# Seven block products in place of eight in two gate/up groups of each FFN, with the weight sums split between VectorE and accumulating DMAs

## The chip, the cores and the metric

The kernel runs on one NeuronCore of a Trainium2 chip. The metric is the device time of one execution in microseconds (us); a run's time is the median of its executions. Engines: TensorE (PE; its weight loads are a row of their own, PEld), VectorE (DVE), ScalarE (ACT), GpSimd (POOL) and SyncE (SP), which only issues DMAs here. Each takes its instructions in a fixed order from a queue of its own. PE writes to PSUM; the others work on SBUF, and DVE and ACT read PSUM too.

## The reference

A decoder trunk of two layers on x of 256 tokens x 1024, in float32:

```
f = swiglu(rms_norm(h, g0)); h = h + 0.5 * rms_norm(f, g1)
h = h + rms_norm(mix(rms_norm(h, g2)), g3)      # layer 0: pooling mixer, layer 1: windowed attention
f = swiglu(rms_norm(h, g4)); h = h + 0.5 * rms_norm(f, g5)
swiglu(h) = (silu(h @ w_gate) * (h @ w_up)) @ w_down     # w_gate, w_up: 1024 x 2816, w_down: 2816 x 1024
```

So there are four FFNs, each read once from HBM. K and V for the attention are projected from h after layer 0.

## The kernel before, in words

The 256 tokens are two row blocks i of 128. Activations are held transposed (`aT`: 8 chunks of 128 of the model dimension, 256 tokens). To keep float32 precision in the fast matmul format (fp32r), each operand is split in two halves: hi, the value cast to fp32r, and lo, the rest. Each product of 128x128 with 128x512 is then three matmuls: hi·hi, hi·lo, lo·hi.

**Weights** arrive as a stream of *units* of 128x1024 float32 (512 KB), in the order of use. `load_unit` (L84) issues the DMA on SP into one of four `raw` buffers, ACT casts the unit to hi (L92), and DVE subtracts to get lo (L93), both into one of eight `hl` buffers. A buffer is free for the next unit when the last matmul that reads it has ended. Everything else on ACT and DVE stands in the same queues between these casts.

**An FFN** (`ffn`, L211) has gate and up in five *groups* of 512 columns and a sixth of 256. A plain group takes gate, 4 units, and up, 4 units: per unit and row block 6 matmuls, so 96 in all. Group 0 comes first: in the first FFN unit by unit for both row blocks, in the others (L250) row block 0 with all eight units and then row block 1. For groups 1 to 4, gate goes to the two `gu` banks of PSUM and up to `acc` banks; `gate` (L216) is silu on ACT, `up` (L221) the product with it on DVE, and `turn` (L226) transposes it on PE (four transposes) and splits it into hi and lo for the down projection. The down projection then takes 22 units, 12 matmuls each; the last six (`TAIL`) are done for row block 0 first, so that its norms begin while PE still works on row block 1.

**A boundary** (`Bound`, L302) follows: `post` (L159) scales the sum by its norm and adds it to h, `norm` (L189) makes the next input, and `transposed` (L175) brings it into the next aT by 8 transposes per row block, ACT's cast (L183) and DVE's subtraction (L184). The power for a norm runs on POOL (L156). PE goes on with row block 0's next matmuls while row block 1 is normalised.

The order on each engine is set by a scheduler when the kernel is built, from the code and its dependences, not by the order of the code alone; each engine then keeps to it.

Of the kernel before, what the change touches and what calls it, by code (L numbers as in the profile page):

```python
# [19 lines left out]
P = 128  # L20
# [7 lines left out]
TAIL = 6  # L28
WARM = 64
CAST = 1024  # L30
# [17 lines left out]
def trunk_kernel(ctx: ExitStack, tc: tile.TileContext, x, pos, gains, pscale, ws, wq, invf, amask, pmat, icnt, out):  # L48
# [6 lines left out]
    s8p = ctx.enter_context(tc.tile_pool(name="s8p", bufs=6))  # L55
# [25 lines left out]
    unit_no = [0]  # L81
    last = {}

    def load_unit():  # L84
        u = unit_no[0]
        unit_no[0] += 1
        raw = rawp.tile([P, 1024], F32, tag="raw", name=f"raw{u}")
        last["dma"] = nc.sync.dma_start(raw, ws[u])
        hl = hlp.tile([P, 2, 1024], F32R, tag="hl", name=f"hl{u}")
        for c in range(0, 1024, CAST):  # L90
            w = slice(c, c + CAST)
            nc.scalar.copy(hl[:, 0, w], raw[:, w])  # L92
            last["dve"] = nc.vector.tensor_sub(hl[:, 1, w], raw[:, w], hl[:, 0, w])  # L93
        return hl

    def load_q_unit(u):
        raw = rawp.tile([P, 1024], F32, tag="raw", name=f"rawq{u}")
        nc.sync.dma_start(raw[:, :768], wq[u])
        hl = hlp.tile([P, 2, 1024], F32R, tag="hl", name=f"hlq{u}")
        nc.scalar.copy(hl[:, 0, :768], raw[:, :768])  # L100
        nc.vector.tensor_sub(hl[:, 1, :768], raw[:, :768], hl[:, 0, :768])
        return hl
# [72 lines left out]
    def transposed(i, src, dst, name):  # L175

        for b in range(2):
            tp = tpp.tile([P, 4, P], F32, tag="tp", name=f"tp_{name}{i}{b}")
            for c in range(4):
                k = b * 4 + c  # L180
                nc.tensor.transpose(tp[:, c], src[:, k * P : (k + 1) * P], ident)
            d = dst[:, :, b * 4 : b * 4 + 4, i * P : (i + 1) * P]
            nc.scalar.copy(d[:, 0], tp)  # L183
            nc.vector.tensor_sub(d[:, 1], tp, d[:, 0])  # L184

# [25 lines left out]
    def ffn(n, aT, boundary, middle=None):  # L211

        h2 = [s8p.tile([P, 2, 4, S], F32R, tag="s8", name=f"h2_{n}_{c}") for c in range(NG + 1)]
        act, prod = {}, {}

        def gate(c, i, g):  # L216
            w = g.shape[-1]
            act[c, i] = sc2.tile([P, 512], F32, tag="w2", name=f"s_{n}_{c}{i}")
            nc.scalar.activation(act[c, i][:, :w], g, AF.Silu)

        def up(c, i, u):  # L221
            w = u.shape[-1]
            prod[c, i] = sc2.tile([P, 512], F32, tag="w2", name=f"m_{n}_{c}{i}")
# [11 lines left out]
        def both(ps, units, c=None):  # L235

            for q in range(4):
                for i in range(2):
                    proj_mm(ps[i], aT, i, units, 512, only=q)
                if c is not None and q < 2:  # L240
                    turn(c, q)

        units = [load_unit() for _ in range(8 - len(first_units))]
        units, first_units[:] = first_units + units, []
# [11 lines left out]
        for c in range(1, NG):  # L256
            units = [load_unit() for _ in range(4)]
            ps = [gup.tile([P, 512], F32, tag="gu", name=f"g_{n}_{c}{i}") for i in range(2)]
            both(ps, units, c - 1)
            for i in range(2):  # L260
                gate(c, i, ps[i])
            units = [load_unit() for _ in range(4)]
            ps = acc_pair(f"u{n}{c}")
            both(ps, units)
            for i in range(2):
                up(c, i, ps[i])
            if c == 2 and middle is not None:
                middle()
        units = [load_unit() for _ in range(4)]
        ps = [gup.tile([P, 512], F32, tag="gu", name=f"g_{n}_{NG}{i}") for i in range(2)]  # L270
        both(ps, units, NG - 1)
        for i in range(2):
            gate(NG, i, ps[i][:, 0:256])
            up(NG, i, ps[i][:, 256:512])

# [7 lines left out]
        for c in range(NF - TAIL):  # L283
            u = load_unit()
            down(c, 0, u)
            down(c, 1, u)
            if c < 2:
                turn(NG, c, 2)
        tail = [load_unit() for _ in range(TAIL)]
# [12 lines left out]
    class Bound:  # L302


        def __init__(self, n, post_idx, half, pre_idx):
            self.n, self.half, self.idx = n, half, (post_idx, pre_idx)

        def prepare(self):
            self.gpost = load_gain(self.idx[0], "post")
            self.gpre = load_gain(self.idx[1], "pre")  # L310
            self.aT = new_aT(self.n)

# [6 lines left out]
        def third(self, i):  # L319
            transposed(i, self.y, self.aT, self.n)  # L320
# [7 lines left out]
    aT = new_aT("x")  # L328
    with tc.manual_schedule(engines={mybir.EngineType.DVE, mybir.EngineType.Activation}):
        y = norm(0, gpre, "x")  # L330
        first_units += [load_unit()]
        nc.sync.dma_start(h[1], x[P:, :])
        transposed(0, y, aT, "x")
        rs = row_rstd(1, "x")
        first_units += [load_unit()]
        y = norm(1, gpre, "x", rs, False)
        first_units += [load_unit()]
        transposed(1, y, aT, "x")
        first_units += [load_unit()]
# [33 lines left out]
    ffn(0, aT, go, rope_tables)  # L373
# [3 lines left out]
    go = Bound("m0", 3, False, 4)  # L377
# [4 lines left out]
    ic = s8p.tile([P, 4, S], F32, tag="s8", name="ic")  # L382
    with in_turn("dma"):
        nc.sync.dma_start(ic, icnt.to_broadcast([P, 4, S]))
    pm = s8p.tile([P, 2, 4, S], F32R, tag="s8", name="pm")
    for si in range(2):
        raw = rawp.tile([P, 1024], F32, tag="raw", name=f"rawpm{si}")
        nc.sync.dma_start(raw, pmat[si])
        nc.vector.tensor_copy(pm[:, si], raw.rearrange("p (g t) -> p g t", g=4))
    u_hl = [s8p.tile([P, 2, D], F32R, tag="s8", name=f"u{i}") for i in range(2)]  # L390
    units = [load_unit() for _ in range(8)]
# [47 lines left out]
    wg += [load_unit() for _ in range(2)]  # L439
# [324 lines left out]
```

## Time and profile before

| | |
|---|---|
| median of 3 timed runs | 992.54 us (991.7 to 993.55) |
| the profiled execution | 995.63 us |
| its span, first to last instruction | 993.7 us |
| busy: PE, DVE, ACT, POOL | 975.3, 575.0, 484.4, 23.2 us |
| moved by DMA | 180.38 MB |

The profile is one execution. "Busy" counts time in instructions; a row of a group gives line, engine, operation, written tile<-read tiles, shape, count, then busy us, mean ns of one, and the idle time of the engine just before them with what ended it. A chain or a timeline gives start and length in us.

### The profile page before, as it was taken

The page shows a single profiled execution, that of the slowest core. Times are in us where ns is not written, and L with a number is a line of the kernel's source. Part 1 is how long each engine was busy: PE and PEld are TensorE (multiplying, and loading weights), DVE is VectorE, ACT ScalarE, POOL GpSimd, SP SyncE. Part 2 cuts the span into 40 slices and gives each one's busy share as a digit, 9 for nine tenths or more (in the row PEclk, how much of TensorE's full clock was granted, in tenths as well). Part 3 has the DMA queues.
Part 4 walks back from the last instruction along what each step waited for, and adds up shares of the span by engine and source line. Part 5 has one row for each costly group of instructions (what it writes and reads, how often), then busy time and mean ns, then how long its engine had stood idle before and what let it go on. Part 6 is the DMA issues. An engine that isn't in the chain of part 4 may idle for free.

```text
span 993.7 us, 12240 instructions
## 1 busy us (share of the span) xinstructions
PE 975.3 (98%) x4664; PEld 810.1 (82%) x4664; DVE 575.0 (58%) x725; ACT 484.4 (49%) x660; POOL 23.2 (2%) x34
## 2 busy tenths in 40 slices
PE   7999999999999999999999999999999999999997
PEld 6888888878788888877888888788898888888886
DVE  5665554578765555447665554685556466555542
ACT  5644443365564444346554443554455565444431
POOL 0000000010100000000000000100000000000000
PEclk8999999999999999999999999999999899999999
DMA  6855655666465575535755756474533137556531
GB/s 224 292 185 188 228 186 189 203 193 213 145 218 185 190 233 180 191 127 174 263 188 171 231 179 197 150 244 154 152 124 128 44 100 260 191 181 203 188 127 42
DMA packets 53722, 180.38 MB, mean 182 GB/s; under 512 B 7265, under 2 KB 7265, under 8 KB 53665
## 3 DMA queue, kind: packets, MB, share of 16 engines
q1 hardware_dynamic: 53584, 179.35, 55.4%
q8 instruction: 36, 0.59, 0.2%
q0 software_dynamic: 80, 0.26, 0.1%
q14 instruction: 22, 0.17, 0.1%
HBM read 178.54 MB, written 1.05 MB: 181 GB/s over the span
## 4 chain that ended last, share of the span: by engine, by line
PE 88%; DVE 4%; issue 3%; ACT 2%; POOL 2%; DMA 1%; SPq 0%; POOLq 0%; DVEq 0%; ACTq 0%
PE g L105 22%; PE acc_d L105 21%; PE acc_u L105 19%; PE acc_b L105 7%; PE vp L105 3%; PE qp L105 3%; PE kp L105 3%; PE htp L230 2%; PE ob L105 1%; PE acc_w L105 1%; PE acc_o L105 1%; DVE h L171 1%; DVE hl L93 1%; ACT hl L92 1%; PE sc L105 1%
## 5 line engine op out<-in xcount | busy, mean ns | idle before, releaser
L93 DVE TENSOR_TENSOR hl<-raw,hl 128x1024 fp32r<-128x1024 f32 x310 | 378.5, 1224 | 298.8 <-ACT hl L92 296.7
L92 ACT CAST hl<-raw 128x1024 fp32r<-128x1024 f32 x310 | 325.5, 1051 | 338.5 <-PE acc_d L105 101.1
L105 PE MATMUL acc_d<-hl,h 128*128 128x512 f32 x1056 | 242.9, 390 | 0.0
L105 PEld LDWEIGHTS acc_d<-hl,h 128*128 128x128 f32 x1056 | 197.4, 188 | 40.7
L105 PE MATMUL g<-hl,aT_m 128*128 128x512 f32 x480 | 116.1, 394 | 0.0
L105 PEld LDWEIGHTS g<-hl,aT_m 128*128 128x128 f32 x480 | 88.6, 188 | 17.8
L105 PE MATMUL acc_u<-hl,aT_m 128*128 128x512 f32 x384 | 88.3, 389 | 0.0
L105 PEld LDWEIGHTS acc_u<-hl,aT_m 128*128 128x128 f32 x384 | 72.1, 188 | 15.0
L105 PE MATMUL acc_u<-hl,aT_f 128*128 128x512 f32 x288 | 67.2, 390 | 0.0
L105 PEld LDWEIGHTS acc_u<-hl,aT_f 128*128 128x128 f32 x288 | 53.8, 188 | 11.5 <-DVE aT_f L184 0.5
L105 PE MATMUL g<-hl,aT_f 128*128 128x512 f32 x240 | 58.7, 395 | 0.0
L105 PE MATMUL g<-hl,aT_x 128*128 128x512 f32 x240 | 58.1, 394 | 0.0
L105 PEld LDWEIGHTS g<-hl,aT_x 128*128 128x128 f32 x240 | 44.3, 188 | 8.9
L105 PEld LDWEIGHTS g<-hl,aT_f 128*128 128x128 f32 x240 | 44.2, 188 | 8.7
L105 PE MATMUL acc_b<-hl,aT_m 128*128 128x512 f32 x192 | 45.3, 392 | 0.1
L105 PE MATMUL acc_u<-hl,aT_x 128*128 128x512 f32 x192 | 44.2, 389 | 0.0
L105 PEld LDWEIGHTS acc_u<-hl,aT_x 128*128 128x128 f32 x192 | 36.0, 188 | 7.5
L105 PEld LDWEIGHTS acc_b<-hl,aT_m 128*128 128x128 f32 x192 | 35.7, 188 | 7.8 <-DVE aT_m L184 0.5
L105 PE MATMUL qp<-hlq,aT_f 128*128 128x384 f32 x192 | 39.1, 346 | 0.0
L105 PE MATMUL kp<-hl,aT_hk 128*128 128x512 f32 x144 | 34.5, 394 | 0.0
L105 PEld LDWEIGHTS qp<-hlq,aT_f 128*128 128x128 f32 x192 | 32.7, 188 | 0.4
L105 PE MATMUL vp<-hl,aT_hk 128*128 128x512 f32 x144 | 33.1, 390 | 0.0
(158 smaller groups left out, 831.3 us busy)
## 6 DMA issues: line engine op xcount, KB each, us to landing
raw<-in_ws SPq DMA_DIRECT2D x310, 512.0 KB, 3.5
rawq<-in_wq SPq DMA_DIRECT2D x16, 384.0 KB, 3.6
gain_post<-in_gains SPq DMA_DIRECT2D x14, 256.0 KB, 4.6
gain_pre<-in_gains SPq DMA_DIRECT2D x12, 256.0 KB, 5.6
rawpm<-in_pmat SPq DMA_DIRECT2D x2, 512.0 KB, 4.7
out_dram<-h SPq DMA_DIRECT2D x4, 256.0 KB, 2.1
h<-in_x SPq DMA_DIRECT2D x2, 256.0 KB, 3.0
h<-in_x SPq DMA_DIRECT2D x1, 512.0 KB, 8.5
```

What stands on the lines that cost most here:

```text
L92: nc.scalar.copy(hl[:, 0, w], raw[:, w])
L93: last["dve"] = nc.vector.tensor_sub(hl[:, 1, w], raw[:, w], hl[:, 0, w])
L105: nc.tensor.matmul(o, l, r, start=start, stop=stop)
L171: nc.vector.scalar_tensor_tensor(h[i][:, c], y[:, c], rs, h[i][:, c], op0=ALU.mult, op1=ALU.add)
L230: nc.tensor.transpose(tp[:, k], prod[c, i][:, k * P : (k + 1) * P], ident)
```

## The change

**The products.** For groups 1 and 3, gate and up of 512 columns are seen as a matrix of 2x2 blocks (rows: the two halves of the model dimension; columns: gate and up), and aT as one of 2x2 blocks (the two row blocks, the two halves). The 2x2 product takes 7 block products instead of 8, with sums of weight blocks and of aT blocks as operands. A block product is 12 matmuls of 128x512; a group takes 84 instead of 96. A `pair` is such a group c and the plain group c+1, whose gate and up are done between the products, two blocks of units at a time.

**The weight sums.** The blocks x, y, z, w (128x2048, 1 MB) give x, x+y, x+y+z, z, y+z, w and x+w (signs are in the stored weights and the sums of aT). x stays in its buffer and is added to in place. The first two sums are DVE additions; sums 2 (y += z) and 3 (x += w) are DMAs from SBUF to SBUF on POOL's queue with an add at the destination. Each operand is cast by ACT and DVE like any block. x and y have two buffers of their own (`xyp`).

**The sums of aT** (`Sums`): four sums of 128x512 with hi and lo, made at the boundary from the transposes in PSUM; they take an `aT` buffer.

**Sizes.** Loads, casts and subtractions go by blocks of two units (128x2048, 1 MB): `raw` 3 blocks (4 units before), `hl` 3 blocks (8 units before). The last group's h2 and other tiles move to half-size buffers. The first four units keep parts of 1024. `kv_input` moves from after group 2 to after the last group (`late`). The stored order of the weights follows. The core of the diff:

```diff
-    rawp = ctx.enter_context(tc.tile_pool(name="rawp", bufs=4))
-    hlp = ctx.enter_context(tc.tile_pool(name="hlp", bufs=8))
+    rawp = ctx.enter_context(tc.tile_pool(name="rawp", bufs=3))
+    xyp = ctx.enter_context(tc.tile_pool(name="xyp", bufs=2))
+    hlp = ctx.enter_context(tc.tile_pool(name="hlp", bufs=3))
...
+    def halves(raw, parts=1, n=1024):
+
+        hl = hlp.tile([P, 2, 2, 1024], F32R, tag="hl", name="hl")
+        for k in range(parts):
+            u = slice(k * (2 // parts), (k + 1) * (2 // parts))
+            nc.scalar.copy(hl[:, 0, u, :n], raw[:, u, :n])
+            last["dve"] = nc.vector.tensor_sub(hl[:, 1, u, :n], raw[:, u, :n], hl[:, 0, u, :n])
+        return [hl[:, :, j] for j in range(2)]
...
+        def product(ps, a, units, start):
+
+            for k in range(4):
+                u = units[k // 2][:, :, (k % 2) * 512 : (k % 2) * 512 + 512]
+                for n, (z, v) in enumerate(((0, 0), (0, 1), (1, 0))):
+                    nc.tensor.matmul(
+                        ps,
+                        a(z, k),
+                        u[:, v],
+                        start=start and k == 0 and n == 0,
+                        stop=k == 3 and n == 2,
+                        skip_group_check=not start,
+                    )
...
+        def add(dst, src, k):
+            if k in DMA_SUMS:
+                nc.gpsimd.dma_start(dst, src, accum_op=ALU.add)
+            else:
+                nc.vector.tensor_add(dst, dst, src)
+
+        def pair(c, turns):
+
+            x, y = [load_raw(1, xyp, "xy") for _ in range(2)]
+            z = load_raw()
+            px = bank()
+            product(px, plain(0, 0), halves(x), True)
+            p1 = temp("p1")
+            nc.scalar.copy(p1, px)
+            add(x, y, 0)
+            py = bank()
+            product(py, summed(0), halves(x), True)
+            p5 = temp("p5")
+            nc.scalar.copy(p5, py)
+            turns[0]()
+            g = [gup.tile([P, 512], F32, tag="gu", name=f"g_{n}_{c}{i}") for i in range(2)]
+            us = load_units(2)
+            both(g, us + us, (0, 1))
+            add(x, z, 1)
+            product(px, summed(1), halves(x), False)
+            u1 = temp("u1")
+            nc.scalar.copy(u1, px)
+            turns[1]()
+            us = load_units(2)
+            both(g, us + us, (2, 3))
...
+            product(py, summed(3), halves(z), False)
+            c01 = temp("c01")
+            nc.vector.scalar_tensor_tensor(c01, py, -1.0, u1, op0=ALU.mult, op1=ALU.subtract)
+            add(y, z, 2)
+            product(px, summed(2), halves(y), False)
+            c11 = temp("c11")
+            nc.vector.scalar_tensor_tensor(c11, px, -1.0, p5, op0=ALU.mult, op1=ALU.subtract)
+            w = load_raw()
+            pz = bank()
+            product(pz, plain(0, 1), halves(w), True)
+            nc.vector.tensor_add(p1, pz, p1)
+            gate(c, 0, p1)
+            up(c, 0, c01)
+            add(x, w, 3)
+            product(px, plain(1, 1), halves(x), False)
+            gate(c, 1, px)
+            up(c, 1, c11)
...
+        pair(1, [lambda: turn(0, 0), lambda: turn(0, 1)])
...
+        pair(3, [turns12, lambda: turn(2, 1)])
```

What this does to the order, at three places. First DVE at the boundary from the first FFN to the mixer, row block 0 (y: post-norm, n: pre-norm, ms: the sum for a norm's power, hl<-raw: a weight's lo half, aT: the next input's). Before:

```order
L171 SCALAR_TENSOR_TENSOR h_94<-y_f_1532,rs_pf_1530,h_94 128x512 x2
L194 TENSOR_TENSOR n_f_1546<-h_94,gain_pre_1167 128x512 x2
L93 TENSOR_TENSOR hl_1675<-raw_1673,hl_1675 128x1024
L154 SCALAR_TENSOR_TENSOR ms_qf_1542<-ss_qf_1537 128x1
L93 TENSOR_TENSOR hl_1680<-raw_1678,hl_1680 128x1024
L195 TENSOR_SCALAR n_f_1546<-n_f_1546,rs_qf_1544 128x512
L93 TENSOR_TENSOR hl_1685<-raw_1683,hl_1685 128x1024
L93 TENSOR_TENSOR hl_1690<-raw_1688,hl_1690 128x1024
L184 TENSOR_TENSOR aT_f_1170<-tp_f_1551,aT_f_1170 128x4x128
```

And now:

```order
L184 SCALAR_TENSOR_TENSOR h_100<-y_f_1421,rs_pf_1419,h_100 128x512 x2
L246 TENSOR_TENSOR n_f_1435<-h_100,gain_pre_1111 128x512 x2
L103 TENSOR_TENSOR hl<-raw_1551,hl 128x2048
L167 SCALAR_TENSOR_TENSOR ms_qf_1431<-ss_qf_1426 128x1
L247 TENSOR_SCALAR n_f_1435<-n_f_1435,rs_qf_1433 128x512
L103 TENSOR_TENSOR hl<-raw_1556,hl 128x2048
L197 TENSOR_TENSOR aT_f_1114<-tp_f_1440,aT_f_1114 128x4x128
```

The same steps in the same order; the weight halves between them are two of 2048 columns, where there were four of 1024, one of them whole between the pre-norm and ms.

Second, PE at the same boundary (tp: the transposes, of row block 0 and then 1; acc_u: the mixer's first projection; pp: its pooling). Before:

```order
L105 MATMUL acc_u_1703<-hl_1675,aT_f_1170 128x512 x6
L105 MATMUL acc_u_1703<-hl_1680,aT_f_1170 128x512 x6
L105 MATMUL acc_u_1704<-hl_1685,aT_f_1170 128x512 x5
L105 MATMUL acc_u_1704<-hl_1690,aT_f_1170 128x512 x6
L181 MATMUL tp_f_1629<-ident,n_f_1624 128x128 x4
L181 MATMUL tp_f_1636<-ident,n_f_1624 128x128 x4
```

And now:

```order
L194 MATMUL tp_f_1440<-ident,n_f_1435 128x128 x4
L194 MATMUL tp_f_1447<-ident,n_f_1435 128x128 x4
L118 MATMUL acc_d_1118<-hl,h_0_5_291 128x512
L118 MATMUL acc_u_1571<-hl,aT_f_1114 128x512 x24
L118 MATMUL acc_u_1572<-hl,aT_f_1114 128x512
L118 MATMUL pp_1660<-pm,u_1549 128x256
L118 MATMUL pp_1674<-pm,u_1549 128x256
L118 MATMUL acc_u_1572<-hl,aT_f_1114 128x512 x2
L194 MATMUL tp_f_1518<-ident,n_f_1513 128x128 x4
L194 MATMUL tp_f_1525<-ident,n_f_1513 128x128 x4
```

Row block 1's transposes now stand behind 27 matmuls of row block 0 and two of the pooling; before there were 36 ahead of them.

Third, DVE at the end of the first pair (raw_584: w; xy_410: x+w; raw_629 and raw_665: the plain blocks of up; xy_724: the next pair's x; c, p, m: see the diff, m being the product with silu). This work has no place in the kernel before, where a group's end on DVE was

```order
L93 TENSOR_TENSOR hl_660<-raw_658,hl_660 128x1024
L224 TENSOR_TENSOR m_10_556<-acc_u_506,s_10_482 128x512
L224 TENSOR_TENSOR m_11_558<-acc_u_507,s_11_484 128x512
L93 TENSOR_TENSOR hl_665<-raw_663,hl_665 128x1024
```

and is now

```order
L103 TENSOR_TENSOR hl<-raw_584,hl 128x2048
L354 SCALAR_TENSOR_TENSOR c_0_564<-st_435,u_0_507 128x512
L103 TENSOR_TENSOR hl<-xy_410,hl 128x2048
L358 SCALAR_TENSOR_TENSOR c_0_582<-st_416,p_0_451 128x512
L103 TENSOR_TENSOR hl<-raw_629,hl 128x2048
L362 TENSOR_TENSOR p_0_432<-st_586,p_0_432 128x512
L103 TENSOR_TENSOR hl<-raw_665,hl 128x2048
L499 CAST posf<-pi_278 128x2
L103 TENSOR_TENSOR hl<-xy_724,hl 128x2048
L280 TENSOR_TENSOR m_0_605<-c_0_564,s_0_603 128x512
```

The product m, which PE's next turn transposes, stands behind the half of the next pair's x.

More of the change, by code (lines that the diff above doesn't have):

```diff
@@ L233, in turn, with both, bank @@
             nc.vector.tensor_sub(d[:, 1], tp[:, :nt], d[:, 0])
-        def both(ps, units, c=None):
-            for q in range(4):
+        def both(ps, units, qs=range(4)):
+            for q in qs:
                 for i in range(2):
                     proj_mm(ps[i], aT, i, units, 512, only=q)
[L240 to L244, printed above, removed]
+        def bank():
+            return accp.tile([P, 512], F32, tag="acc", name=f"st{n}")
@@ L511, in trunk_kernel @@
     for g in range(3):
-        units = [load_unit() for _ in range(4)]
+        units = load_units(4)
         for i in range(2):
@@ L521, in trunk_kernel @@
     for g in range(3):
-        units = [load_unit() for _ in range(4)]
+        units = load_units(4)
         for i in range(2):
@@ L622, in trunk_kernel @@
             values(1, 1)
-    units = [load_unit() for _ in range(4)]
+    units = load_units(4)
     scores(1, 2, gup, "gu")
```

243 lines of the change are left out of this document (156 added, 87 removed).

## Prediction

> **What bounds the kernel now.** I read the page first (parts 1, 2, 4 and 5).
>
> ```profile
> span 993.7 us, 12240 instructions
> ...
> PE 975.3 (98%) x4664; PEld 810.1 (82%) x4664; DVE 575.0 (58%) x725; ACT 484.4 (49%) x660; POOL 23.2 (2%) x34
> ...
> PEclk8999999999999999999999999999999899999999
> ...
> PE 88%; DVE 4%; issue 3%; ACT 2%; POOL 2%; DMA 1%; SPq 0%; POOLq 0%; DVEq 0%; ACTq 0%
> ...
> L93 DVE TENSOR_TENSOR hl<-raw,hl 128x1024 fp32r<-128x1024 f32 x310 | 378.5, 1224 | 298.8 <-ACT hl L92 296.7
> L92 ACT CAST hl<-raw 128x1024 fp32r<-128x1024 f32 x310 | 325.5, 1051 | 338.5 <-PE acc_d L105 101.1
> ```
>
> PE is busy for 975.3 of 993.7 us and carries 88% of the chain that ended last. ACT's casts of the weights wait for PE to give a buffer back, and the subtractions on VectorE (DVE) wait for the casts: both run behind PE. So fewer matmuls are worth their full time, as long as the other engines still keep up everywhere. Next, the chain in order of time inside the second FFN, and one stretch of it by engine (busy us and instructions of PE, PEld, DVE, ACT, POOL, then clock, DMA share, GB/s).
>
> ```profile
> 284.72 2.73 PE g L105 x12
> 287.89 2.79 PE g L105 x12
> 291.11 5.46 PE g L105 x24
> 296.57 10.88 PE acc_u L105 x48
> ```
>
> ```profile
> 296.57:342.00 45.43, 45.43 (x209) 37.60 (x209) 24.41 (x24) 20.95 (x24) 0.00 (x0) 1.00 0.56 187
> ```
>
> A 128x512 matmul passes in 5.46/24 = 0.2275 us, twelve in 2.73. Between the first two pieces lie 287.89 - 284.72 - 2.73 = 0.44 us: one turn (four transposes). In these 45.43 us, two groups long, PE never pauses; DVE works 24.41 us and ACT 20.95.
>
> **What is removed.** Each pair takes 7 products of 12 matmuls for the 96 of a plain group: 12 fewer. Two pairs in four FFNs: 96 x 0.2275 = **-21.8 us**, all on the path. Nothing else leaves PE.
>
> **What DVE and ACT get.** I need prices of 128x2048 instructions, which the trace lacks; I extend them from two lengths.
>
> ```profile
> L184 DVE TENSOR_TENSOR aT_f<-tp_f,aT_f 128x512 fp32r<-128x512 f32 x12 | 7.7, 684 | 2.9 <-ACT aT_f L183 2.9
> L183 ACT CAST aT_f<-tp_f 128x512 fp32r<-128x512 f32 x12 | 6.4, 584 | 0.6 <-PE tp_f L181 0.6
> L219 ACT ACTIVATE s<-g 128x512 f32<-128x512 f32 (+1 forms) x40 | 22.2, 555 | 21.9 <-PE g L105 21.8
> ```
>
> DVE: 684 ns for 512 columns and 1224 for 1024, so 540 more per 512 and 2.30 us for 2048. ACT: 584 and 1051, so 1.99 us. A pair casts 7 blocks of products and 4 plain ones: DVE 11 x 2.30 + two sums of 2.30 + seven short operations and some four turns of 0.68 = 37 us, ACT 11 x 1.99 + about 11 short ones of 0.58 = 28 us. PE needs 180 x 0.2275 + 4 x 0.44 = 42.7 us. DVE is then 87% busy: no bound by itself, but three hl buffers (six units, eight before) leave little slack, so I follow the pair step by step.
>
> **Inside a pair** (us from its first product, no stall assumed). PE: x 0 to 2.7, x+y to 5.5, turn, first plain block to 11.4, x+y+z to 14.1, turn, second plain block to 20.0, z to 22.7, y+z to 25.4, w to 28.2, one matmul, x+w, 23 matmuls, turn at 36.4. A cast may start when the product three blocks back has ended. w: cast behind two silu (20.0 + 0.56), to 22.5, DVE to 24.8, wanted at 25.4. Then c01 to 25.5, the half of x+w (cast from 22.7) to 27.8, c11 to 28.5; but x+w writes the bank that c11 reads, and PE is there at 28.4: stall 0.1. Then DVE has one block to 30.8, p1 to 31.5, one block to 33.8, the next x to 36.1, and the product of c01 and silu to 36.8, which the turn wants at 36.4: stall 0.4. Together 0.5 in 8 pairs: **+4 us**, between 0 (the scales are a few per cent off) and +8.
>
> **Entering a pair.** In FFNs two to four the fourth block of group 0 waits for the first one's buffer until row block 1 has used it, so casts bunch when the pair begins: x+y+z and the second plain block follow each other on ACT at 2 x 1.99 us, where PE has one block of 5.46 us less what it is late. I find PE out of work for some 1.3 us: 3 x 1.3 = **+4 us**, between 1 and 6.
>
> **The two sums by DMA.** No row shows an accumulating DMA. The nearest:
>
> ```profile
> raw<-in_ws SPq DMA_DIRECT2D x310, 512.0 KB, 3.5
> qT<-in_amask POOLq DMA_DIRECT2D x1, 256.0 KB, 5.0
> ```
>
> and the stretch of the first 25 us, 40 slices of GB/s:
>
> ```profile
> GB/s 0 0 3 180 344 321 236 144 177 167 243 347 383 403 419 419 419 419 419 406 229 105 170 334 315 66 39 184 269 374 39 0 85 315 354 53 26 26 177 393
> ```
>
> So the engines move at most 419 GB/s, 2.5 us per MB. A 1 MB load lands in 3.5 + 1.25 = 4.75 us. A sum issued from POOL takes, read once, 5.0 + 0.79/0.419 = 6.9 us; read twice, 5.0 - 0.6 + 5.0 = 9.4; with the two loads that are then in flight taking half of the engines, 11.9. By the Trainium skill ("Collectives: The Full Stack", the bandwidth ceiling) an add in a DMA needs two source reads and so halves the rate (1.93 measured there): by that alone a sum would take some 9.2 us, an estimate, as in the middle case; no run here shows it yet.
>
> y+z has time: it starts when x+y is done, before the pair begins, and is wanted at 14.6. x+w is tight: w's load starts when the first plain block's half is done (DVE does x+y and x+y+z around it: 4.3 to 6.6), lands at 9 to 11.4, and the sum must land by 22.7: 11.3 to 13.7 us for 6.9 to 11.9. I take 0.5 us late per pair: **+4 us**, from 0 to +12; worse is a rival.
>
> **Row boundaries.** Here 2048-wide casts stand where 1024-wide ones stood, on the chain post-norm, pre-norm, transposes. Boundary FFN one to mixer, of before, DVE then PE (start, busy, ..., [idle before <-releaser]), with POOL's power:
>
> ```profile
> 198.20 1.22 DVE L93 TENSOR_TENSOR hl<-raw,hl 128x1024 fp32r<-128x1024 f32 x1
> 199.33 0.15 DVE L154 SCALAR_TENSOR_TENSOR ms_qf<-ss_qf 128x1 f32<-128x1 f32 x1
> ...
> 201.07 0.49 DVE L195 TENSOR_SCALAR n_f<-n_f,rs_qf 128x512 f32<-128x512 f32 x1 [0.44 <-POOL rs_qf L156]
> 201.47 2.52 DVE L93 TENSOR_TENSOR hl<-raw,hl 128x1024 fp32r<-128x1024 f32 x2
> 203.90 1.28 DVE L184 TENSOR_TENSOR aT_f<-tp_f,aT_f 128x512 fp32r<-128x512 f32 x2
> ...
> 212.09 0.49 DVE L195 TENSOR_SCALAR n_f<-n_f,rs_qf 128x512 f32<-128x512 f32 x1 [0.44 <-POOL rs_qf L156]
> ```
>
> ```profile
> 197.14 1.04 ACT L92 CAST hl<-raw 128x1024 fp32r<-128x1024 f32 x1
> 198.08 0.62 ACT L152 ACTIVATE jk_qf<-h 128x512 bf16<-128x512 f32 x1
> ```
>
> ```profile
> 201.70 1.06 PE L181 MATMUL tp_f<-ident,n_f 128*128 128x128 f32 x8 [0.65 <-DVE n_f L195]
> 202.52 1.40 PE L105 MATMUL acc_d<-hl,h 128*128 128x512 f32 x5
> 203.76 8.69 PE L105 MATMUL acc_u<-hl,aT_f 128*128 128x512 f32 x36
> 212.72 1.06 PE L181 MATMUL tp_f<-ident,n_f 128*128 128x128 f32 x8 [0.26 <-DVE n_f L195]
> 213.54 8.43 PE L105 MATMUL acc_u<-hl,aT_f 128*128 128x512 f32 x36
> ```
>
> ACT's cast at 197.14 becomes 1.99 long, jk_qf ends at 199.9, the half of that block holds DVE until 201.5, and only then comes ms_qf (199.33 before). POOL and the way to L195 took 201.07 - 199.33 = 1.74; so L195 starts at 203.2, PE transposes from 203.7 to 204.7 (its tail is through at about 202.2), and behind one more 2.30 us half DVE delivers the first aT at 206.4. PE can do two matmuls before that: row block 0 starts 206.4 - 0.5 - 203.76 = 2.2 us late. Row block 1 follows: its L195 at 213.4 for 212.09, behind another block. But PE now has only 25 matmuls ahead of those transposes, to 211.7, then two of the pooling whose input ACT casts after the normalisation (214.0), then the transposes, to 215.9. Before, 36 were done at 213.54; now 27 and 0.4 us of pooling: (215.9 - 213.54) + 9 x 0.2275 - 0.4 = 4.0 us late. Mixer to FFN two and FFN two to three have the same order of casts (24 to 27 matmuls ahead of the second transposes): 3.2 and 3.5 by the same working. Attention to FFN four still has 36 ahead: 1.2. Sum **+12 us**; at least 4 x 1.2 = 5, at most 4 x 4 = 16. FFN three to the K projections needs no aT at once: nothing.
>
> **The rest.** The mixer, K, V and Q held eight units and hold six: I take +2 (0 to +5). At nothing I cost these. The four sums of aT: their first reader comes after group 0's 22 us of PE; uncovered they would cost some 5 us a boundary. The start: same 1024-wide steps. `kv_input`, moved to the head of the down projections: a block of two units there gives DVE 5.46 us of PE time for 2.30 us of work. SP's queue: the next pair's x stands ahead of raw loads, but takes y's buffer, free at 18.9 us of the pair, so nothing behind it is held; if it took x's own (27.8), the turn would wait some 3 us more. POOL's queue: between the sums of a pair stands nothing, and the powers of the norms come long after the last sum.
>
> **Sum.** -21.8 + 4 + 4 + 4 + 12 + 2 = +4.2 us. The profiled execution took 995.63 us (the span of 993.7 and 1.9 around it), the three timed runs have their median at 992.54, 3.1 lower; on that median: 992.5 + 4.2 = **996.7, so 997 us**.
>
> **Rivals.** (1) *Cover holds: faster.* All edges at the low ends: -21.8 + 0 + 1 + 0 + 5 + 0 = -16; with half of the way from there to my values, -6. So 977 to 990, around 983. For it: PE waits only 0.26 and 0.65 us at these very transposes, and DVE's idle 298.8 us is cover that my step by step may have used too sparingly. Against: 24.41 us of DVE work per 45 become 37. It decides at boundaries of 2 us instead of 3 to 4.
> (2) *The accumulating DMA is the bound: slower.* Place: x+w in each pair; from 12 to 13 us per sum PE stands still for every further us, eight times. At 16 us per sum: 8 x 3.5 = 28 us in place of my 4, so 1021. A longer stop costs more than itself, as the start of the span shows (PE; then the stretch by engine, the clock third from the end):
>
> ```profile
> 10.26 1.09 PE L181 MATMUL tp_x<-ident,n_x 128*128 128x128 f32 x8 [3.65 <-DVE n_x L195]
> ```
>
> ```profile
> 12.00:18.00 6.00, 5.73 (x11) 3.57 (x12) 5.23 (x9) 3.76 (x8) 0.55 (x1) 0.50 0.60 204
> ```
>
> After 3.65 us without work PE has a granted clock of 0.50 for these 6 us, which loses 3 us. At 20 us per sum it would be 8 x (7.5 + 3) = 84 us: 1077. The stops that I forecast, 2.3 us at the longest, stay under that length. The Trainium skill ("TensorE: Matmul & The Clock Gate", part 1) puts the limit at an idle window of about 3.4 us, after which the clock is halved until some 3.4 us of steady work: by that, too, my sum pays nothing for the clock, and the trace agrees with 3.65 us. For it: no row gives its price, and 5.0 us for 256 KB from POOL is already slow beside 3.5 for 512 KB from SP. Against: y+z shows a slack of ten us, and the engines move 187 of 419 GB/s here. The Trainium skill ("SBUF — State Buffer", who interferes with whom) says that a VectorE instruction with two SBUF inputs holds up GpSimd instructions that read SBUF, not those that only write it, as writing descriptors does; by that DVE's load alone would not make this rival true. No run shows it yet.
> (3) *Nothing in sum*: edges of 20 to 24 us, 990.6 to 994.5.
>
> **How the numbers follow.** My sum, slower: 0.36, its own range 994.6 to 1006. Rival 1: 0.39. Rival 2: 0.14. Rival 3: 0.11. A measurement of this kernel tells about 0.2% (2 us) from no change. Slower: 0.36 + 0.14 = 0.50; same 0.11; faster 0.39. Range: from 977 (low end of rival 1) to 1025 (rival 2 at 16 to 17 us).
>
> **What would show it.** PE should have 4568 matmuls and about 953 us of busy time. Right if PE's idle time before the norms' transposes and the first products with aT is 2 to 4 us per boundary, if the turn in the last product's block waits half a us, and if POOL's sums land 9 to 12 us after issue. Wrong if PE's idle time grows by under 15 us in all (rival 1), or if st products wait for the cast of xy behind a POOL DMA by several us (rival 2); and wrong in its foundation if the matmuls themselves pass slower than 0.2275 us.

## The result, and the profile after

The changed kernel takes **1005.83 us** (median; 1003.88 to 1006.43), the one before 992.48 beside it (991.7 to 993.55): a ratio of 1.013, 95% interval 1.0113 to 1.0148, so 1.3% slower: 13.4 us. The two profiled executions, which everything below compares, differ by less, 10.0 us in span, because that of the kernel before (995.63 us) took 3.1 us more than its median; that of the kernel after took 1005.53 us. Page of the kernel after, parts 1, 2, 5 and 6:

```profile
span 1003.7 us, 11391 instructions
...
PE 966.1 (96%) x4568; PEld 793.8 (79%) x4568; DVE 673.0 (67%) x659; ACT 531.8 (53%) x591; POOL 37.7 (4%) x50
...
PEclk8999999999799999999999999999999989999999
...
L103 DVE TENSOR_TENSOR hl<-raw,hl 128x2048 fp32r<-128x2048 f32 (+1 forms) x141 | 318.1, 2259 | 198.4 <-ACT hl L102 198.1
L102 ACT CAST hl<-raw 128x2048 fp32r<-128x2048 f32 (+1 forms) x141 | 265.7, 1886 | 196.4 <-PE acc_d L118 106.3
...
xy<-raw POOLq DMA_DIRECT2D x16, 1024.0 KB, 8.2
```

The 96 matmuls are gone, but PE's busy time fell by only 9.2 us of the expected 21.8, and its idle time rose from 18.4 to 37.6 us. The clock row has a new dip in its eleventh slice, at about 260 us: there matmuls ran at half clock, and half-clock matmuls count as busy (over the whole span this is 7 us at the most, see below). So busy share alone hides the loss. I cut PE's timeline where the first instruction of a stage starts, and took lengths (us); the last two columns are experiments told below. In the kernel after, one product matmul of FFN four runs before the last 22 of its group 0; I cut behind these.

| stage on PE | before | after | two steps | six single |
|---|---|---|---|---|
| start, FFN one's gate and up | 141.7 | 136.3 | 135.9 | 137.0 |
| FFN one's down projection, mixer up to its output projection | 90.6 | 96.4 | 92.2 | 91.7 |
| that projection, group 0 of FFN two | 52.3 | 60.5 | 53.6 | 53.2 |
| FFN two, the other groups | 102.7 | 99.8 | 97.2 | 97.7 |
| its down projection, group 0 of FFN three | 85.8 | 90.0 | 88.0 | 86.7 |
| FFN three, the rest | 166.8 | 163.8 | 161.6 | 161.4 |
| K and V | 69.7 | 69.1 | 70.0 | 69.8 |
| Q, attention, group 0 of FFN four | 114.8 | 123.1 | 123.7 | 115.1 |
| FFN four, the other groups | 102.7 | 97.7 | 97.2 | 97.6 |
| its down projection | 66.7 | 67.0 | 67.1 | 66.9 |
| span | 993.7 | 1003.7 | 986.5 | 976.9 |

Each of the four rows with the other groups should fall by 24 matmuls, 5.46 us; they fall by 5.4, 2.9, 3.0 and 5.0, so 5.5 us are lost there. Most of the time is lost at the four boundaries: 5.8 + 8.3 + 4.2 + 8.3 = 26.6 us. The entry to FFN two, first PE in the kernel before:

```profile
258.82 1.09 PE L181 MATMUL tp_m<-ident,n_m 128*128 128x128 f32 x8 [0.62 <-DVE n_m L195]
259.67 1.41 PE L105 MATMUL acc_w<-hl,yT 128*128 128x512 f32 x5
260.92 8.72 PE L105 MATMUL acc_b<-hl,aT_m 128*128 128x512 f32 x36
```

And in the kernel after: PE, DVE, POOL, and the stretches behind PE's stop (the clock is the third number from the end).

```profile
242.69 17.84 PE L118 MATMUL acc_w<-hl,yT 128*128 128x512 f32 x77
263.63 1.97 PE L194 MATMUL tp_m<-ident,n_m 128*128 128x128 f32 x8 [3.10 <-DVE n_m L247]
267.29 8.86 PE L118 MATMUL acc_b<-hl,aT_m 128*128 128x512 f32 x25 [1.69 <-ACT aT_m L196]
```

```profile
257.94 2.29 DVE L103 TENSOR_TENSOR hl<-raw,hl 128x2048 fp32r<-128x2048 f32 x1 [0.79 <-ACT hl L102]
260.15 0.15 DVE L167 SCALAR_TENSOR_TENSOR ms_qm<-ss_qm 128x1 f32<-128x1 f32 x1
260.36 2.29 DVE L103 TENSOR_TENSOR hl<-raw,hl 128x2048 fp32r<-128x2048 f32 x1
263.09 0.49 DVE L247 TENSOR_SCALAR n_m<-n_m,rs_qm 128x512 f32<-128x512 f32 x1 [0.44 <-POOL rs_qm L169]
```

```profile
260.38 2.68 POOL L169 TENSOR_TENSOR rs_qm<-ms_qm,nhalf 128x1 f32<-128x1 f32 x1 [5.88 <-DVE ms_qm L167]
```

```profile
264.00:267.00 3.00, 1.60 (x8) 1.20 (x6) 1.49 (x2) 3.00 (x6) 0.00 (x0) 0.50 0.96 401
267.00:270.00 3.00, 2.71 (x6) 1.88 (x7) 3.00 (x5) 1.58 (x4) 0.09 (x1) 0.50 0.17 30
270.00:273.00 3.00, 3.00 (x8) 2.32 (x8) 2.87 (x5) 1.76 (x5) 0.46 (x1) 0.50 0.80 320
273.00:276.00 3.00, 3.00 (x14) 2.39 (x14) 0.67 (x3) 0.72 (x1) 0.55 (x1) 0.94 0.00 0
```

One half of 2.29 us stands ahead of ms, the next one between ms and L247. From ms to L247 it is 263.09 - 260.15 = 2.94 us; before it was 1.72. PE stops 3.10 us where it stopped 0.62, then 1.69 more for ACT's aT behind a 2048-wide cast, and then 25 matmuls take 8.86 us in place of 5.7, with a granted clock of 0.50.

At the mixer PE's longest stop is that of the two pooling matmuls, which now stand ahead of row block 1's transposes; their input, cast by ACT, stands behind the normalisation that waits for the power:

```profile
208.58 0.80 PE L118 MATMUL pp<-pm,u 128*128 128x256 f32 x2 [2.79 <-ACT u L542]
```

The pairs, by contrast, wait little. All that PE waits for VectorE there is in the waits of PE:

```profile
PE st L305 <- DVE c L358: 1.2, 2, 0.6
```

and 0.3 us for a turn. The sums made by DMA land 8.2 us after issue in the median of 16, but the slowest, the x+w of the second pairs in FFNs two to four, took 12.6 to 13.3 us. ACT's cast waited for these three, and the two stops for c11 stand behind two of them. The chain in FFN two, on POOL, ACT, DVE and PE:

```profile
347.56 0.86 POOL L322 DMA_DIRECT2D xy<-raw  x1 [13.82 <-DMA raw<-in_ws]
```

```profile
360.93 1.91 ACT L102 CAST hl<-xy 128x2048 fp32r<-128x2048 f32 x1 [1.70 <-DMA xy<-raw]
```

```profile
362.88 2.29 DVE L103 TENSOR_TENSOR hl<-xy,hl 128x2048 fp32r<-128x2048 f32 x1 [0.71 <-ACT hl L102]
365.09 0.69 DVE L358 SCALAR_TENSOR_TENSOR c<-st,p 128x512 f32<-128x512 f32 x1
```

```profile
365.83 3.03 PE L305 MATMUL st<-hl,aT_m 128*128 128x512 f32 x12 [0.62 <-DVE c L358]
```

So a late sum cost PE some 0.6 us, twice.

### The profile page after: what moved, and what is told of

Same layout as the page of the kernel before. It is cut to its first block, busy times and chain, and to the rows that moved or that the text cites. A ratio compares the mean times of both kernels' runs of the same rounds, so it can differ in the third digit from the quotient of the medians.

```text
span 1003.7 us, 11391 instructions
## 1 busy us (share of the span) xinstructions
PE 966.1 (96%) x4568; PEld 793.8 (79%) x4568; DVE 673.0 (67%) x659; ACT 531.8 (53%) x591; POOL 37.7 (4%) x50
## 5 line engine op out<-in xcount | busy, mean ns | idle before, releaser
L103 DVE TENSOR_TENSOR hl<-raw,hl 128x2048 fp32r<-128x2048 f32 (+1 forms) x141 | 318.1, 2259 | 198.4 <-ACT hl L102 198.1
L102 ACT CAST hl<-raw 128x2048 fp32r<-128x2048 f32 (+1 forms) x141 | 265.7, 1886 | 196.4 <-PE acc_d L118 106.3
L103 DVE TENSOR_TENSOR hl<-xy,hl 128x2048 fp32r<-128x2048 f32 x40 | 91.6, 2290 | 18.6 <-ACT hl L102 18.3
L102 ACT CAST hl<-xy 128x2048 fp32r<-128x2048 f32 x40 | 76.6, 1915 | 40.8 <-DVE xy L324 28.5
L118 PE MATMUL g<-hl,aT_m 128*128 128x512 f32 x288 | 70.3, 395 | 0.5 <-DVE m L280 0.3
L305 PE MATMUL st<-hl,S_m 128*128 128x512 f32 x192 | 46.5, 391 | 0.0
L118 PE MATMUL u<-hl,aT_m 128*128 128x512 f32 x192 | 45.9, 391 | 0.0
L305 PEld LDWEIGHTS st<-hl,S_m 128*128 128x128 f32 x192 | 35.8, 188 | 8.0 <-DVE hl L103 0.6
L118 PEld LDWEIGHTS u<-hl,aT_m 128*128 128x128 f32 x192 | 35.8, 188 | 7.4 <-ACT hl L102 0.2
L118 PE MATMUL qp<-hl,aT_f 128*128 128x384 f32 x192 | 39.7, 347 | 0.0
L118 PE MATMUL g<-hl,aT_x 128*128 128x512 f32 x144 | 34.8, 395 | 0.0
```

The costliest lines, as they stand in the source:

```text
L102: nc.scalar.copy(hl[:, 0, u, :n], raw[:, u, :n])
L103: last["dve"] = nc.vector.tensor_sub(hl[:, 1, u, :n], raw[:, u, :n], hl[:, 0, u, :n])
L118: nc.tensor.matmul(o, l, r, start=start, stop=stop)
L305: nc.tensor.matmul(ps, a(z, k), u[:, v], start=start and k == 0 and n == 0, stop=k == 3 and n == 2, skip_group_check=not start,)
```

## The experiments

**Theory**: the boundaries lose the time, because casts and subtractions of 2048 columns stand on the chain of the norms. **Rivals**: the smaller window of hl buffers, freed two units at a time; the products with their sums of aT; the accumulating DMAs. Each kernel was timed beside the one before (992.7 to 992.8 us). In each the scheduler ordered the instructions anew, so orders differ a little beside the edit.

**1. Two steps of 1024 in a block** (changed kernel; buffers, loads, products as they are).

```diff
-        for k in range(parts):
-            u = slice(k * (2 // parts), (k + 1) * (2 // parts))
+        for k in range(2):
+            u = slice(k, k + 1)
```

> The changed kernel (1005.8 us) with every block of two units cast and subtracted in two steps of 1024 columns instead of one of 2048; loads, buffers, products and sums as they are. Theory (length): the loss at the row boundaries is the length of the 2048-wide steps on VectorE (2.29 us, 1.22 for 1024) in front of the norm's short steps and beside POOL's power, which spans 0.55 us alone and 2.46 to 2.68 us beside such a step. Then most of the 26 us lost at the boundaries come back: PE's idle time falls from 37.6 to 20 to 26 us, no power spans over 1.5 us, the granted clock keeps 0.9 or more at the entry to FFN two, and the time is 985 to 994. Rival (buffers): six units held in three blocks, freed two at a time, instead of eight freed one at a time, starve PE of weights; the time stays within 4 us of 1005.8. Rival (sums of aT): the work of the sums at the boundaries is the loss; the time stays within 2 us.

Measured: **986.45 us** (986.33 to 988.3), ratio 0.9941 (0.9929 to 0.9954): 19.4 us back, and faster than the kernel before. The theory's range held; PE's idle time is 986.5 - 960.0 = 26.5 us, just above its 20 to 26. The same place on PE in this kernel:

```profile
253.76 1.09 PE L194 MATMUL tp_m<-ident,n_m 128*128 128x128 f32 x8 [0.63 <-DVE n_m L247]
254.61 2.33 PE L118 MATMUL acc_w<-hl,yT 128*128 128x512 f32 x9
256.78 5.83 PE L118 MATMUL acc_b<-hl,aT_m 128*128 128x512 f32 x25
263.81 0.73 PE L118 MATMUL acc_b<-hl,aT_m 128*128 128x512 f32 x2 [1.20 <-DVE hl L103]
```

The stop is 0.63 us, as before the change, and nine matmuls of acc_w still cover the way back to the first aT; 25 matmuls take 5.83 us. Most of what is left stands in the row that ends with the entry to FFN four (123.7 us in the table), with this stop:

```profile
804.34 0.73 PE L118 MATMUL acc_b<-hl,aT_m 128*128 128x512 f32 x2 [2.96 <-DVE hl L103]
```

It waits for a weight, not for the norm. The third block of group 0 needs the hl block that the o projection's last twelve matmuls read; when these end, the post-norm begins as well, and VectorE does the weight's second half only behind it (PE, then VectorE):

```profile
793.99 2.97 PE L118 MATMUL acc_o<-hl,oT 128*128 128x512 f32 x12
```

```profile
798.44 1.23 DVE L103 TENSOR_TENSOR hl<-raw,hl 128x1024 fp32r<-128x1024 f32 x1 [0.25 <-ACT hl L102]
...
803.07 1.21 DVE L103 TENSOR_TENSOR hl<-raw,hl 128x1024 fp32r<-128x1024 f32 x1
```

That spoke for the window as the second cause. The row holds more than this entry, though. Cut once more at row block 0's first transposes, the entry takes 28.5 us before, 37.2 in the kernel after, 34.8 here and 31.3 in experiment 6; Q and the attention ahead of it take 86.3, 85.9, 88.9 and 83.8. In that first part the granted clock fell to 0.50 before (787 to 793 us of the span) and here (765 to 771), and stayed at 1.00 in the kernel after and in experiment 6.

**2. Plain groups in the new blocks** (changed kernel with four plain groups in place of the pairs; no sums of aT, no sums of weights, the weights stored in the plain order).

```diff
-        pair(1, [lambda: turn(0, 0), lambda: turn(0, 1)])
...
-        pair(3, [turns12, lambda: turn(2, 1)])
+        for c in range(1, NG):
+            units = load_units(4)
...
-            self.sums = Sums(self.n) if self.want else None
+            self.sums = None
```

> The changed kernel with plain groups (96 matmuls) in place of the four kinds of pairs, and without the sums of aT and of weights; blocks of 2048, three hl blocks and three raw blocks kept, the weights stored in the plain order. Theory (length, or buffers): the loss stands in the boundaries and has nothing to do with the products, so the time is the changed kernel's plus the 21.8 us of the removed matmuls, less the 5 us that the pairs lose inside: 1014 to 1026. Rival (products and sums): without them the kernel is the one before in larger blocks, 992 to 998.

Measured: **1019.79 us** (1017.93 to 1019.98), ratio 1.0267 (1.0252 to 1.0282). The products and the sums of aT are not the main cause: without them the stop at FFN two is the same to 0.01 us, and cut by stage 23.4 of the 26.6 us at the boundaries remain.

```profile
249.91 17.84 PE L117 MATMUL acc_w<-hl,yT 128*128 128x512 f32 x77
270.85 1.10 PE L193 MATMUL tp_m<-ident,n_m 128*128 128x128 f32 x8 [3.10 <-DVE n_m L246]
274.51 8.01 PE L117 MATMUL acc_b<-hl,aT_m 128*128 128x512 f32 x25 [2.56 <-ACT aT_m L195]
```

**3. All weight sums on VectorE** (changed kernel).

```diff
-DMA_SUMS = (2, 3)
+DMA_SUMS = ()
```

> The changed kernel with all four weight sums of a pair on VectorE, none by an accumulating DMA. Theory: the DMAs land 8.2 us after issue and nobody waits for them, so nothing is gained; VectorE gets 16 more steps of 2.28 us inside the pairs, 1005 to 1016. Rival (accumulating DMA): waits for y+z and x+w, or the DMAs' traffic beside the loads, are part of the loss; 995 to 1003.

Measured: 1010.85 us (1007.31 to 1016.03), ratio 1.0199 (1.0168 to 1.0229): slower, not faster. PE doesn't wait for c11 here at all, and still nothing is gained in the whole. The accumulating DMAs are not the main loss.

**4. Only VectorE in two steps**, and **5. only ACT in two steps** (changed kernel).

```diff
             nc.scalar.copy(hl[:, 0, u, :n], raw[:, u, :n])
-            last["dve"] = nc.vector.tensor_sub(hl[:, 1, u, :n], raw[:, u, :n], hl[:, 0, u, :n])
+            for j in range(u.start, u.stop):
+                v = slice(j, j + 1)
+                last["dve"] = nc.vector.tensor_sub(hl[:, 1, v, :n], raw[:, v, :n], hl[:, 0, v, :n])
```

> The changed kernel with ACT's casts left at 2048 columns and only VectorE's subtractions in two steps of 1024. Theory (length on VectorE): the norm's short steps stand in VectorE's queue behind the halves, so most of what two steps on both engines brought (19.4 us) comes from here: 986 to 993. Theory (length on ACT counts as much): a half can't start before the whole cast of 1.9 us, so the chain cast, subtraction, product stays long: 994 to 1001. Rival (no effect): 1003 to 1006.

```diff
-            nc.scalar.copy(hl[:, 0, u, :n], raw[:, u, :n])
+            for j in range(u.start, u.stop):
+                nc.scalar.copy(hl[:, 0, j, :n], raw[:, j, :n])
```

> The mirror of the run with two subtractions: ACT casts in two steps of 1024, VectorE subtracts 2048 columns in one. Both splits together brought 19.4 us, VectorE's alone 7.3. Theory (what counts is the latency of a whole block, cast and then subtraction, which only both splits let overlap): VectorE's 2048-wide step still stands ahead of the norms and still needs both casts, so this brings less than half, 997 to 1005. Rival (ACT's queue is the place, since its casts stand ahead of the squares and of aT's casts): the missing 12 us come from here, 990 to 996.

Measured: 998.48 us (996.96 to 999.22), ratio 1.0052 (1.0035 to 1.007), and 998.73 us (997.67 to 1000.03), ratio 1.0065 (1.0052 to 1.0078). Each alone brings some 7 us, both 19.4, so in the total my first theory, that VectorE's queue holds most of it, fails. By stage, in the profiled executions, it fails less. At the first three boundaries both splits give back 13.1 us, VectorE's alone 12.2 and ACT's alone 5.4, most of that (4.6) at the entry to FFN two. But with VectorE's alone the row of Q, attention and group 0 of FFN four takes 130.2 us, 7.1 more than in the kernel after, and PE is at half clock there for 17 us:

```profile
764.00:781.00 17.00, 17.00 (x58) 12.86 (x58) 5.40 (x14) 4.73 (x12) 0.00 (x0) 0.51 0.28 107
```

Why the clock fell there in that kernel stays open, so the total of experiment 4 is no clean price of VectorE's steps. With ACT's split alone PE waits 5.90 us for a weight at the entry to FFN four. The likely reason, not tested by itself: a subtraction starts when the whole cast has ended, so with one engine split the other's long step still holds the whole block.

**6. Six buffers of one unit** (changed kernel: the same SBUF for hl, cast, subtracted and freed unit by unit; loads stay 1 MB).

```diff
-    hlp = ctx.enter_context(tc.tile_pool(name="hlp", bufs=3))
+    hlp = ctx.enter_context(tc.tile_pool(name="hlp", bufs=6))
...
-        hl = hlp.tile([P, 2, 2, 1024], F32R, tag="hl", name="hl")
+        hl = []
+        for j in range(2):
+            t = hlp.tile([P, 2, 1024], F32R, tag="hl", name="hl")
...
```

> The changed kernel with the three hl blocks of two units replaced by six buffers of one unit, each cast and subtracted by itself (1024 columns) and freed by itself; loads stay blocks of 1 MB. Beside the kernel with two steps in one block (986.5 us) only the freeing is finer. Theory (length is all but a little): 983 to 987, PE's stops for hl halves at the entry to FFN four (0.70 and 2.96 us there) shortened. Theory (freeing two at a time is what is left of the loss): 976 to 982. Against both: the order that the scheduler then finds is worse, over 988.

Measured: **979.32 us** (978.68 to 982.05), ratio 0.9866 (0.9846 to 0.9887): 1.3% faster than the kernel before, the fastest of all here, by 7.1 us ahead of experiment 1. Not all of that is shown to come from the buffers: in the profiled executions the row up to FFN four is 8.6 us shorter, 3.5 at the entry and 5.1 ahead of it, in the attention, where experiment 1's ran 6 us at half clock. Its page, and PE at the entry to FFN four:

```profile
span 976.9 us, 11896 instructions
...
PE 953.9 (98%) x4568; PEld 789.6 (81%) x4568; DVE 690.9 (71%) x844; ACT 554.4 (57%) x776; POOL 35.2 (4%) x50
...
PEclk7999999999999999999999999999999999999999
```

```profile
789.77 5.60 PE L119 MATMUL acc_b<-hl,aT_m 128*128 128x512 f32 x24
797.43 1.06 PE L195 MATMUL tp_m<-ident,n_m 128*128 128x128 f32 x8 [2.06 <-DVE n_m L248]
```

PE's busy time is the forecast 953, and no dip is left behind the start. Experiment 1 stopped twice for weights there (0.70 and 2.96 us), behind 9 and 6 matmuls; here 24 run in one piece. At the entry to FFN two this kernel has the order of the kernel after, with a shorter half in it (VectorE):

```profile
252.91 0.15 DVE L168 SCALAR_TENSOR_TENSOR ms_qm<-ss_qm 128x1 f32<-128x1 f32 x1
252.98 1.22 DVE L103 TENSOR_TENSOR hl<-raw,hl 128x1024 fp32r<-128x1024 f32 x1
254.64 0.48 DVE L248 TENSOR_SCALAR n_m<-n_m,rs_qm 128x512 f32<-128x512 f32 x1 [0.44 <-POOL rs_qm L170]
```

From ms to L248 it is 1.73 us where it was 2.94, with the same steps in the same order: here the width of the half makes the difference.

**7. The kernel before with six buffers.**

```diff
-    hlp = ctx.enter_context(tc.tile_pool(name="hlp", bufs=8))
+    hlp = ctx.enter_context(tc.tile_pool(name="hlp", bufs=6))
```

> The kernel before with six hl buffers instead of eight, nothing else. Theory (length): the smaller window costs little where the steps are 1024 long, 0 to 5 us (993 to 998), most of it at the entry to FFN four, where units of the o projection hold buffers. Rival (buffers): the window is the loss of the changed kernel, over 10 us (1003 or more).

Measured: 1000.59 us (999.02 to 1001.76), ratio 1.0074 (1.0052 to 1.0095): 7.8 us, between the two expectations. The window has a price of its own.

**8. Plain groups in blocks, four hl blocks** (experiment 2 with the old window).

```diff
-    hlp = ctx.enter_context(tc.tile_pool(name="hlp", bufs=3))
+    hlp = ctx.enter_context(tc.tile_pool(name="hlp", bufs=4))
```

> The plain groups in blocks of 2048 (1019.8 us) with four hl blocks instead of three, so the window of eight units of the kernel before, still freed two at a time. Theory: the smaller window by itself cost 7.8 us in the kernel before, the width of the steps the rest; 1008 to 1014. Rival (width costs nothing once the window is back): 994 to 1000. Rival (only the width counts): 1017 to 1021.

Measured: 1003.74 us (1001.94 to 1004.58), ratio 1.0112 (1.0099 to 1.0125), below the theory's range. So with eight units wide blocks (loads, steps and freeing by two) cost 11 us, and the fourth block is worth 16 us. Width and window are not terms of a sum: 7.8 and 11 make 19, and both together cost 27. One reading, not tested by itself, is that a buffer that is freed late and refilled by a long step is late twice.

**9. The norm's power left out.**

```diff
-        nc.gpsimd.tensor_tensor(rs, ms, nhalf, op=ALU.pow)
+        nc.vector.tensor_scalar(rs, ms, 0.0, 1.0, op0=ALU.mult, op1=ALU.add)
```

> The changed kernel with the power on POOL left out: a 128x1 instruction on VectorE writes 1 in its place, so the norms do not scale. It asks whether the long spans of the power (2.46 to 2.68 us beside a 2048-wide half) are the cause or only lie beside it. Theory (VectorE's queue): the step that waits for the power stands behind the same half in VectorE's own queue, which ends 0.44 us before it, so only some 0.4 us per norm come back, 0 to 4 us in all: 1001 to 1006. Rival (the power's span is the cause): 2 us at each of three places and the low clock behind the longest stop, 994 to 1000.

Measured: 996.88 us (991.86 to 1004.71, ten executions), ratio 1.0048 (1.0017 to 1.0078). That lies in the rival's range, but it is no proof of the rival, since the stand-in on VectorE changed the order as well: at FFN two no half stands between ms and L247 any more. The mean granted clock of its executions went from 0.978 to 0.995, and those from 0.987 up took 992 to 995 us. So it doesn't show whether the power's long span costs anything by itself. A kernel with the power itself on VectorE gave no time, so this rival stays untested.

**10. Filling PE's stop** (changed kernel with twelve matmuls of zeros at the entry to FFN two).

```diff
     def third(self, i):
+            if self.n == "m0" and i == 0:
+                t = tpp.tile([P, 512], F32, tag="tp", name="fill")
+                for _ in range(12):
+                    nc.tensor.matmul(t, zeros, last["jk"], start=True, stop=True)
```

> The changed kernel with twelve extra 128x512 matmuls of zeros (bf16) on PE, which can start when ACT has read h for row block 0's pre-norm at the entry to FFN two; nothing reads their result, all other work is unchanged. They fill PE's stop of 3.10 us there without shortening the chain that it waits for. Theory (the low clock is a part of the loss): the granted clock stays at 1.0 behind the stop, where 25 matmuls took 8.86 us instead of 5.7 and eight transposes 1.97 instead of 1.06; 3 to 5 us come back: 1000 to 1003. Rival (the low clock lies beside other waits and costs nothing of its own): 1005 to 1007.

Measured: 1008.62 us (1004.31 to 1014.35), ratio 1.0177 (1.0144 to 1.0209), outside both ranges: nothing gained. PE there:

```profile
258.67 2.75 PE L466 MATMUL fill<-jk_qm,zeros 128*128 128x512 bf16 x12 [0.31 <-ACT jk_qm L166]
...
263.71 1.10 PE L195 MATMUL tp_m<-ident,n_m 128*128 128x128 f32 x8 [0.45 <-DVE n_m L248]
...
265.11 6.17 PE L118 MATMUL acc_b<-hl,aT_m 128*128 128x512 f32 x25
273.49 0.99 PE L118 MATMUL acc_b<-hl,aT_m 128*128 128x512 f32 x2 [2.20 <-DVE hl L103]
274.50 1.94 PE L195 MATMUL tp_m<-ident,n_m 128*128 128x128 f32 x8
```

The clock held (6.17 us for 25 matmuls, 1.10 for the transposes), but PE then stopped 2.20 us for a weight's half that had been hidden under the slow matmuls, and the clock fell there. My theory of this run fails: at this place the low clock had cover, and its price is not the 3 to 5 us that the slow matmuls suggest. The median itself comes from executions that scatter (see the last section).

## Why the prediction was right or wrong

The direction and the range held. The size did not: +0.45% was forecast, +1.3% measured; +4.2 us against +13.4 by the medians, +10.0 by the spans that the table cuts. On the spans the sum comes out as -21.8 + 5.5 (pairs; 12 forecast) + 26.6 (boundaries; 14 forecast with the rest) - 0.3 elsewhere. The two errors, 6.5 us too much and 12.6 too little, in part make up for each other: that the sum came as near as it did is luck.

- **What is removed, -21.8 us: right.** In experiment 1 FFN two's and FFN four's other groups are 5.5 us shorter, and experiment 6 stands 21.3 us below experiment 7, which has the same window and width of steps. My foundation, 0.2275 us a matmul, held.
- **Entering a pair, +4: too much.** I followed the kernel after against experiment 1 matmul by matmul: after the first 72 or so of the first pair it is 0.61, 0.63 and 0.43 us behind in FFNs two to four, together 1.7 us.
- **Inside a pair, +4, and the sums by DMA, +4: too much.** Together they cost what is left of the 5.5 us, some 3.8. PE stops 1.2 us for c11 in two of the eight pairs and 0.3 for one turn. The late x+w lies behind both stops for c11, so the mechanism that I named for it is there. Its landing 12.6 to 13.3 us after issue in three pairs is past my 11.9, and it reaches PE where I put the deadline, 11.3 to 13.7 us. **Rival 2**, the sum as the bound, is wrong: the other thirteen landed in 6.9 to 8.9 us. The Trainium skill ("Collectives: The Full Stack", the bandwidth ceiling) gave some 9.2 by its halved rate; the trace has a median of 8.2, with this spread.
- **Row boundaries +12 and the rest +2: this is the step that failed**, with 26.6 us in their place. I forecast 4.0, 3.2, 3.5 and 1.2 us; the rows lost 5.8, 8.3, 4.2 and 8.3. So the entries to FFN two and FFN four hold most of the error. Three parts of the working are to be named. First, "POOL and the way to L195 took 201.07 - 199.33 = 1.74" was held constant, though a half of 1.22 us lay inside that time; with 2.29 it became 2.94 at FFN two. Second, I took FFN four's entry at 1.2 us by counting matmuls ahead of the second transposes, and priced the window at +2 for the mixer, K, V and Q, and at nothing for this entry. The entry itself grew by 8.7 us in the kernel after, with PE waiting 1.50 us for a weight and then 1.94 for the norm; by 6.3 with short steps (experiment 1), where a weight whose buffer the o projection still held ended last; and by 2.8 with single buffers (experiment 6). Third, I wrote that stops of up to 2.3 us "stay under that length" after which the clock is halved. The stops became longer (3.10), and much shorter ones were followed by half clock too, as the last section shows.
- **At nothing: right** for `kv_input` and FFN three to K (-0.5 us in K and V), and nearly for the sums of aT: without them and the products 23.4 of the 26.6 us remain (experiment 2).
- **Rival 1**, that the cover holds, was nearer than my sum in the pairs and false at the boundaries. Experiments 1 and 6, at 986 and 979 us, lie in its range.

What stays open: how much of the 26.6 us is the low clock's own. The mean granted clocks are 0.985 and 0.992; the difference over the span, 0.007 x 1003.7 = 7 us, is the most that it can be, and experiment 10 shows that part of it has cover.

## What to carry to other kernels

When a change makes steps wider to save instructions, look for the short steps of other chains in the same queues: each waits for a whole wide step on both engines, and a duration read off the trace that contains such a step must be scaled with it. Count buffers by when each is freed, not by their bytes: the same SBUF, as six single units in place of three double ones with the steps split, was worth 26.5 us here, 19.4 of them with the split steps alone. Where matmuls are saved and time is not, compare PE stage by stage, since idle time and half-clock matmuls stand in different columns.

## What the runs showed of the hardware

**POOL's power stretches with VectorE's step beside it.** It spans 0.55 us alone, 1.40 to 1.47 beside a 1024-wide subtraction, and 2.46 to 2.68 beside a 2048-wide one, ending some 0.4 us after it. The Trainium skill ("SBUF — State Buffer", who interferes with whom) says that VectorE and GpSimd share a pair of ports under an exclusive lock; these spans agree. The prediction cited it for the DMA sums, and overlooked it where it applied.

**The clock fell after stops much shorter than 3.65 us.** In the kernel after, PE stopped 1.60 us among the small matmuls of the attention, and some 2 us later the clock was at one half (PE's row, then the stretch):

```profile
804.00 1.10 PE L118 MATMUL ob<-kv,qT 128*128 128x64 f32 x8 [1.60 <-ACT qT L711]
```

```profile
806.00:809.00 3.00, 2.59 (x7) 2.04 (x7) 1.32 (x3) 1.35 (x3) 0.00 (x0) 0.50 0.66 227
```

So it was after the mixer's stop of 2.79 us (0.51 from 209 to 212 us) and experiment 1's of 2.96 (0.50 from 806 to 809). But in experiment 4 the same stop of 1.60 us was followed by

```profile
798.00:801.00 3.00, 3.00 (x20) 2.70 (x21) 3.00 (x5) 1.42 (x4) 0.00 (x0) 1.00 0.00 0
```

and experiment 6's stop of 2.06 us by 1.00 as well. In the attention of experiment 4, where the clock stood at one half for 17 us, the longest wait just before was 1.02 us. So in these runs the length of a single stop doesn't tell whether the clock falls. One program can differ from execution to execution: experiment 10's six took 1004.31 to 1005.33 us at a mean clock of 0.992 and 1011.91 to 1014.35 at 0.980 to 0.983. The Trainium skill ("TensorE: Matmul & The Clock Gate", part 1) speaks of a free-running window of about 3.4 us; such a scatter fits a free-running window, but my reading of it as the length that a stop must have does not hold here.

**An accumulating DMA of 1 MB within SBUF**, issued by POOL beside the loads, landed in 8.2 us (median of 16, from 6.9 to 13.3); POOL itself was busy some 0.9 us for each. Why three took over 12 us is open; in FFN two the DMA engines were busy to 0.90 of the time meanwhile (347.5 to 361 us).
